# A diffusion layer in fp32 halves: merge's and the output projection's matmuls tied into one order, with some groups of four K tiles out of turn

## The chip, the cores and the metric

The kernel runs on one core of one Trainium2 chip. The metric is the device time of one execution in microseconds (us), as the median of the runs shown. TensorE is PE in what follows (PEld is its weight loads), VectorE is DVE, ScalarE is ACT, GpSimd is POOL, and SyncE's queue of transfers is SP.

## The reference, cut to what matters

One layer over 256 latent tokens and 256 context tokens of width 2048. Its attention branches give `ya` and `yb` (256 x 1024 each); the part that the change touches is the merge and the output projection:

```
g_a, g_b = split(sigmoid(h @ w_gate + b_gate), 2)
mix = (g_a * (ya @ w_proj_gla) + g_b * (yb @ w_proj_diff)) @ w_out
x_new = x + g1 * mix
h2 = modulate(rms_norm(x_new, norm2_w), sh2, sc2)
x_new = x_new + g2 * conv_ffn(h2)          # w_up, conv, silu gate, w_down
```

All of it is fp32. `w_proj_gla` and `w_proj_diff` are 1024 x 2048, `w_out` is 2048 x 2048, `w_up` 2048 x 11264, `w_down` 5632 x 2048.

## The kernel before, in words

Activations lie transposed (128 features by 256 tokens) and are split into a high half, rounded to TensorE's fp32r type, and a low half, the rest. Weights come from HBM in pieces of 128 x 1024 (`fetch`, L225, four buffers `wraw`); `split` (L199) makes of each 128 x 512 the halves `whi` (a copy on ACT, L206) and `wlo` (a subtraction, L213, on DVE or now and then on POOL), four buffers of each. One such 128 x 512 holds four K tiles: a group.

`col_tile` (L238) computes one column tile: 128 output features by 256 tokens, summed over its K tiles. For each K tile there are two matmuls: h (L262), the weight's high half against both halves of the activation (512 columns), and l (L264), the weight's low half against the activation's high half (256 columns). A group of four K tiles has eight matmuls in one of three orders:

```
TURN = "h0 l0 h1 l1 h2 l2 h3 l3".split()
ENDED = "h0 l0 h1 l1 h2 l2 l3 h3".split()
SHIFTED = "h0 h1 l0 h2 l1 h3 l2 l3".split()
```

The instructions are written in program order and a scheduler then sets the order on each engine by its own estimate of times. Where `col_tile` is given orders, its matmuls are tied: each is held behind the one before it in one chain (`chain`, L265 to L268), so that the scheduler can't mix two column tiles. Without orders all groups are TURN but the last, which is ENDED, and the scheduler may move matmuls of the next tile ahead. Before the change only the up and down projections (tiles named `upg`, `upv`, `down`) are tied; out of turn are there the groups of column tiles 8 to 16 of `w_up` and 0 to 2 of `w_down`.

The stages around the change, in order:

- The gates (`gate_tile`), 32 column tiles of `w_gate`, not tied.
- The merge, L1090 to L1107: 16 columns, each with two column tiles of 8 K tiles, `pga` (against `ya`) and `pgb` (against `yb`). ACT copies half of a finished bank to `pt` (L273), DVE adds the other half (L274), the result is multiplied with the gate (L1101, on DVE for `pga`, on POOL for `pgb`), and a column later `merged` adds both (L1086) and splits the sum into the halves of `A[c]` (L231 on ACT, L232 on DVE). The tiles `a0` to `a15` are these `A[c]`.
- The output projection, L1128 to L1152: 16 column tiles `mix` of 16 K tiles. Each needs all of `a0` to `a15`, so its last K tile waits for the last `merged`.
- `up0`, six column tiles of `w_up` side by side (`up`, L1177 to L1179), not tied, while `normed` (L1165 to L1167) makes the new `a0` to `a15`; then `upg` and `upv` column tiles, 41 of each, with the convolution (L1211 to L1214), the gate's silu and product (L1221, L1222) for each pair; then 16 `down` tiles.

Between all this DVE computes modulation vectors: 128 x 1024 pieces of `w_ada` (`araw`, two buffers, transfers issued at L332 on SP) are multiplied with a vector and summed, one dot of L338 each. In the merge there are 12 of them for 16 columns. SP issues all weight transfers in one order.

Of the kernel before, what the change touches and what calls it, by code (L numbers as in the profile page):

```python
# [146 lines left out]
def layer_kernel(tc, I, out):  # L147
# [3 lines left out]
    with es:  # L151
# [82 lines left out]
        TURN = "h0 l0 h1 l1 h2 l2 h3 l3".split()  # L234
        ENDED = "h0 l0 h1 l1 h2 l2 l3 h3".split()
        SHIFTED = "h0 h1 l0 h2 l1 h3 l2 l3".split()

        def col_tile(src, acts, b, orders=None):  # L238

            nk = src.shape[1]
            nq = nk // 4
            tied = orders is not None
            orders = orders or [TURN] * (nq - 1) + [ENDED]
            for k0 in range(0, nk, 8):
                kn = min(8, nk - k0)
                if k0:  # L250
                    flush()
                raw = fetch(src[:, k0:k0 + kn, :].rearrange("p a b -> p (a b)"), kn * P)
                for kk in range(0, kn, 4):
                    whi, wlo = split(raw[:, kk * P:(kk + 4) * P], 4 * P)
                    order = orders[(k0 + kk) // 4]
                    for which in order:
                        j = int(which[1])
                        k = k0 + kk + j
                        sl = slice(j * P, (j + 1) * P)
                        first, last = k == 0 and which == "h0", k >= nk - 4 and which == order[-1]  # L260
                        if which[0] == "h":
                            i = PE.matmul(b.rearrange("p (a b) -> p a b", a=2), whi[:, sl], acts[k], start=first, stop=last)  # L262
                        else:
                            i = PE.matmul(b[:, T:], wlo[:, sl], acts[k][:, 1, :], start=False, stop=last)  # L264
                        if tied:  # L265
                            if chain:
                                after(i, chain[0])
                            chain[:] = [i]  # L268
                    if k0 and not kk:
                        flush(latest)  # L270
# [32 lines left out]
        A, B, C = [], [], []  # L303
# [785 lines left out]

        for c in range(KT):  # L1090
            ba, bb = acc_bank("pga"), acc_bank("pgb")
            col_tile(I["w_proj"][c, :, 0:8, :], yap, ba)
            col_tile(I["w_proj"][c, :, 8:16, :], ybp, bb)
            for j in (c, 16 + c):
                sigs.append(S.activation(gates[j], gates[j], AF.Sigmoid))
                after(sigs[-1], sigm)
                after(sigs[-1], copied[0])
            for b, j in ((ba, c), (bb, 16 + c)):
                t = p3.tile([P, T], F32, tag="pt", bufs=2, name="pt")
                i = added(t, b)  # L1100
                (G if j > c else V).tensor_tensor(gates[j], t, gates[j], op=ALU.mult)  # L1101
                if j == c and c:
                    merged(c - 1, i)
            ada_next(12 / 16)
# [24 lines left out]
        for c in range(KT):  # L1129
            b = acc_bank("mix")  # L1130
            if c < half:
                ada_next(1)
            col_tile(I["w_out"][c], A, b)
            if c == half:
                ada_done(16)
                ada_done(32)
                V.tensor_scalar(a2, adav[:, 32:48], 1.0, None, op0=ALU.add)
                V.tensor_tensor(a2, a2, vcol("norm2", 0, 16), op=ALU.mult)
                V.tensor_scalar(a2, a2, -0.5 / D, None, op0=ALU.mult)
            xr = p3.tile([P, T], F32, tag="xr", bufs=2, name="xr")  # L1140
            nc.scalar.dma_start(xr, I["xl"][:, c, :])
            x1.append(C[c][:, 0, :])
            V.scalar_tensor_tensor(xr, b[:, :T], adav[:, c:c + 1], xr, op0=ALU.mult, op1=ALU.add)
            i = V.scalar_tensor_tensor(x1[c], b[:, T:], adav[:, c:c + 1], xr, op0=ALU.mult, op1=ALU.add)
            if c >= half:
                for k in range(2 * (c - half), 2 * (c - half) + 2):
                    unnormed(k, i, summed)
            sq = p3.tile([P, T], F32, tag="sq2" if c else "sq_sum", bufs=2 if c else 1, name="sq2")
            S.activation(sq, x1[c], AF.Square)
            if c == 0:  # L1150
                sq_sum = sq
            elif c < KT - 1:  # L1152
                summed = G.tensor_tensor(sq_sum, sq_sum, sq, op=ALU.add)
# [43 lines left out]
        with tc.tile_pool(name="ffn", bufs=1) as pf:  # L1197
# [26 lines left out]
                split_act(g[:, 1, :], g[:, 0, :], ug)  # L1224
                gs.append(g)

            def orders(n, nq, first, last):


                shifted = [i for j in range(0, nq * (last - first + 1) - 3, 7) for i in (first * nq + j, first * nq + j + 4)]  # L1230
                q = range(n * nq, (n + 1) * nq)
                return [ENDED if i == (last + 1) * nq - 1 else SHIFTED if i in shifted else TURN for i in q]

            for j in range(UPS // 2):
                gated(j, ups[2 * j], ups[2 * j + 1])
            for j in range(UPS // 2, FT):
# [9 lines left out]
            for c in range(KT):  # L1246
                b = acc_bank("down")
# [21 lines left out]
```

## Time and profile before

| what | value |
|---|---|
| median of 3 runs (lowest, highest) | 1704.58 us (1703.33, 1706.26) |
| the profiled execution: time, span of its profile | 1705.99 us, 1704.2 us |
| PE, PEld, DVE, ACT, POOL busy | 99%, 86%, 73%, 58%, 22% |
| matmuls | 10460 |
| bytes read from HBM | 364.73 MB |

Lines of a timeline give start, duration, engine, source line, operation, output and inputs, and in brackets the idle time before an instruction and what ended it. Successive matmuls overlap: the pace is read from starts, not from durations. DVE and ACT too start an instruction a little before the one ahead has ended. SPq lines are transfers being issued. In a table of windows each row has a stretch of time, its length, and busy time with the number of instructions for each engine, PE first.

### The profile page before, as it was taken

The page shows a single profiled execution, that of the slowest core. Times are in us where ns is not written, and L with a number is a line of the kernel's source. Part 1 is how long each engine was busy: PE and PEld are TensorE (multiplying, and loading weights), DVE is VectorE, ACT ScalarE, POOL GpSimd, SP SyncE. Part 2 cuts the span into 40 slices and gives each one's busy share as a digit, 9 for nine tenths or more (in the row PEclk, how much of TensorE's full clock was granted, in tenths as well). Part 3 has the DMA queues.
Part 4 walks back from the last instruction along what each step waited for, and adds up shares of the span by engine and source line. Part 5 has one row for each costly group of instructions (what it writes and reads, how often), then busy time and mean ns, then how long its engine had stood idle before and what let it go on. Part 6 is the DMA issues. An engine that isn't in the chain of part 4 may idle for free.

```text
span 1704.2 us, 29160 instructions
## 1 busy us (share of the span) xinstructions
PE 1680.4 (99%) x10460; PEld 1461.5 (86%) x10460; DVE 1236.4 (73%) x2314; ACT 983.8 (58%) x1992; POOL 373.4 (22%) x384
## 2 busy tenths in 40 slices
PE   8999999999999999999999999999999999999999
PEld 6779999897887888888888988888888888888887
DVE  5556665867688988788998797777788777644443
ACT  5324554655355777666666676666666666444443
POOL 0002534545110000001213212222222222222222
PEclk9999999999999999999999999999999999999999
DMA  9995532433667554687787666666776666666664
GB/s 384 407 408 182 173 121 90 136 112 124 197 210 234 169 178 161 216 299 271 259 276 259 182 217 220 223 225 226 231 231 225 224 227 225 202 199 195 200 200 135
DMA packets 108451, 368.75 MB, mean 216 GB/s; under 512 B 12176, under 2 KB 17040, under 8 KB 108304
## 3 DMA queue, kind: packets, MB, share of 16 engines
q1 hardware_dynamic: 103264, 362.51, 63.7%
q10 hardware_dynamic: 5040, 4.37, 0.8%
q8 instruction: 82, 1.34, 0.3%
q14 instruction: 65, 0.53, 0.1%
HBM read 364.73 MB, written 2.10 MB: 215 GB/s over the span
## 4 chain that ended last, share of the span: by engine, by line
PE 90%; DVE 5%; DMA 3%; ACT 1%; issue 1%; POOL 0%; DVEq 0%; ACTq 0%
PE down L262 9%; PE upg L262 8%; PE upv L262 8%; PE gate L262 7%; PE sweep L350 5%; PE down L264 5%; PE upg L264 4%; PE upv L264 4%; PE gate L264 4%; PE mix L262 3%; PE ab L350 2%; DMA araw<-in_w_ada 2%; PE mix L264 2%; PE pga L262 2%; PE pgb L262 2%; PE dk L313 1%
## 5 line engine op out<-in xcount | busy, mean ns | idle before, releaser
L206 ACT CAST whi<-wraw 128x512 fp32r<-128x512 f32 (+2 forms) x1004 | 605.6, 608 | 388.5 <-PE down L262 110.5
L213 DVE TENSOR_TENSOR wlo<-wraw,whi 128x512 fp32r<-128x512 f32 (+2 forms) x849 | 588.7, 703 | 236.8 <-ACT whi L206 228.7
L213 POOL TENSOR_TENSOR wlo<-wraw,whi 128x512 fp32r<-128x512 f32 (+1 forms) x155 | 208.2, 1343 | 644.9 <-ACT whi L206 572.2
L262 PE MATMUL down<-g,whi 128*128 128x512 f32 x704 | 243.6, 392 | 0.0
L262 PE MATMUL upg<-a,whi 128*128 128x512 f32 x656 | 229.4, 392 | 0.0
L262 PE MATMUL upv<-a,whi 128*128 128x512 f32 x656 | 229.3, 392 | 0.0
L264 PE MATMUL down<-g,wlo 128*128 128x256 f32 x704 | 195.4, 280 | 0.7 <-DVE wlo L213 0.7
L264 PE MATMUL upg<-a,wlo 128*128 128x256 f32 x656 | 182.8, 280 | 1.0 <-DVE wlo L213 1.0
L264 PE MATMUL upv<-a,wlo 128*128 128x256 f32 x656 | 182.8, 280 | 0.0
L262 PE MATMUL gate<-a,whi 128*128 128x512 f32 x512 | 179.4, 396 | 0.0
L338 DVE CUSTOM_DVE_ANT_0 araw<-araw,cb 128x1024 f32<-128x1024 f32 x128 | 163.7, 1282 | 15.2 <-DMA araw<-in_w_ada 15.2
L262 PEld LDWEIGHTS down<-g,whi 128*128 128x128 f32 x704 | 131.0, 187 | 28.3
L262 PEld LDWEIGHTS upv<-a,whi 128*128 128x128 f32 x656 | 122.4, 187 | 26.8
L262 PEld LDWEIGHTS upg<-a,whi 128*128 128x128 f32 x656 | 122.4, 187 | 26.7
L264 PE MATMUL gate<-a,wlo 128*128 128x256 f32 x512 | 140.9, 285 | 0.5 <-DVE wlo L213 0.5
L264 PEld LDWEIGHTS down<-g,wlo 128*128 128x128 f32 x704 | 132.9, 189 | 1.9 <-DVE wlo L213 1.0
L264 PEld LDWEIGHTS upg<-a,wlo 128*128 128x128 f32 x656 | 123.9, 189 | 2.2 <-DVE wlo L213 1.6
L264 PEld LDWEIGHTS upv<-a,wlo 128*128 128x128 f32 x656 | 123.9, 189 | 0.5
L262 PEld LDWEIGHTS gate<-a,whi 128*128 128x128 f32 x512 | 94.3, 188 | 19.3 <-issue 0.4
L264 PEld LDWEIGHTS gate<-a,wlo 128*128 128x128 f32 x512 | 96.5, 188 | 6.9 <-issue 1.5
L262 PE MATMUL mix<-a,whi 128*128 128x512 f32 x256 | 88.8, 397 | 0.0
L264 PE MATMUL mix<-a,wlo 128*128 128x256 f32 x256 | 69.3, 281 | 1.0 <-DVE wlo L213 1.0
(332 smaller groups left out, 3346.0 us busy)
## 6 DMA issues: line engine op xcount, KB each, us to landing
wraw<-in_w_up SPq DMA_DIRECT2D x164, 512.0 KB, 4.4
araw<-in_w_ada SPq DMA_DIRECT2D x128, 512.0 KB, 5.0
wraw<-in_w_down SPq DMA_DIRECT2D x80, 512.0 KB, 3.9
ada<-in_w_ad SPq DMA_DIRECT2D x64, 512.0 KB, 9.8
wraw<-in_w_gate SPq DMA_DIRECT2D x64, 512.0 KB, 4.2
wraw<-in_w_in SPq DMA_DIRECT2D x58, 512.0 KB, 3.9
wraw<-in_w_proj SPq DMA_DIRECT2D x32, 512.0 KB, 4.5
wraw<-in_w_out SPq DMA_DIRECT2D x32, 512.0 KB, 4.8
```

Of the source, the lines that this page charges most:

```text
L206: copied[0] = S.copy(hi[:, :n], raw)
L213: i = e.tensor_tensor(lo[:, :n], raw, hi[:, :n].bitcast(F32), op=ALU.subtract)
L262: i = PE.matmul(b.rearrange("p (a b) -> p a b", a=2), whi[:, sl], acts[k], start=first, stop=last)
L264: i = PE.matmul(b[:, T:], wlo[:, sl], acts[k][:, 1, :], start=False, stop=last)
L313: PE.matmul(o, whi[:, sl], hi[k], start=first and j == 0, stop=False)
L338: i = V.tensor_tensor_reduce(raw, raw, cb[:, q * 1024:(q + 1) * 1024], 1.0, 0.0, op0=ALU.mult, op1=ALU.add, accum_out=ada2[:, j, q:q + 1])
L350: return kept(PE.matmul(*args, **kw))
```

## The change

The function `orders`, which so far stood in the part of the up and down projections, moves ahead of `col_tile`, and the merge's and the output projection's column tiles are given orders by it. `orders(n, nq, first, last)` returns the orders of column tile n with nq groups: between the tiles first and last the groups at distances 0, 4, 7, 11, 14 and so on from the first are SHIFTED, the very last group of tile last is ENDED, all others are TURN.

```
-            col_tile(I["w_proj"][c, :, 0:8, :], yap, ba)
-            col_tile(I["w_proj"][c, :, 8:16, :], ybp, bb)
+            col_tile(I["w_proj"][c, :, 0:8, :], yap, ba, orders(2 * c, 2, 2, 18))
+            col_tile(I["w_proj"][c, :, 8:16, :], ybp, bb, orders(2 * c + 1, 2, 2, 18))
...
-            col_tile(I["w_out"][c], A, b)
+            col_tile(I["w_out"][c], A, b, orders(c, 4, 2, 7))
...
+        def orders(n, nq, first, last):
+            shifted = [i for j in range(0, nq * (last - first + 1) - 3, 7) for i in (first * nq + j, first * nq + j + 4)]
+            q = range(n * nq, (n + 1) * nq)
+            return [ENDED if i == (last + 1) * nq - 1 else SHIFTED if i in shifted else TURN for i in q]
```

In the merge this makes groups 4, 8, 11, 15, 18, 22, 25, 29, 32 and 36 of 64 SHIFTED and 37 ENDED; in the output projection groups 8, 12, 15, 19, 22 and 26 of 64 SHIFTED and 31 ENDED. Every column tile so far ended in an ENDED group. No instruction is added or removed; SP's and POOL's orders stay as they were, while those of PE, DVE and ACT change from the first `pga` tile to the first `upg` tiles. In the changed kernel the lines between `col_tile` and the old place of `orders` have numbers higher by 7.

PE at the end of the first output tile. `mix_9955` is column tile 0, `mix_10017` column tile 1; `wlo_10000` and `whi_9999` are tile 0's last group, `a15_1450` its last K tile's activation. Before:

```order
L264 MATMUL mix_9955<-a14_1380,wlo_10000 128x256
L264 MATMUL mix_10017<-a0_219,wlo_10024 128x256
L262 MATMUL mix_10017<-a1_330,whi_10023 128x512
L264 MATMUL mix_10017<-a1_330,wlo_10024 128x256
L262 MATMUL mix_10017<-a2_402,whi_10023 128x512
L264 MATMUL mix_10017<-a2_402,wlo_10024 128x256
L262 MATMUL mix_10017<-a3_481,whi_10023 128x512
L264 MATMUL mix_10017<-a3_481,wlo_10024 128x256
L262 MATMUL mix_10017<-a4_560,whi_10035 128x512
L264 MATMUL mix_9955<-a15_1450,wlo_10000 128x256
L264 MATMUL mix_10017<-a4_560,wlo_10036 128x256
```

The same place in the changed kernel:

```order
L271 MATMUL mix_9955<-a14_1380,wlo_10000 128x256
L269 MATMUL mix_9955<-a15_1450,whi_9999 128x512
L271 MATMUL mix_9955<-a15_1450,wlo_10000 128x256
L269 MATMUL mix_10017<-a0_219,whi_10023 128x512
L271 MATMUL mix_10017<-a0_219,wlo_10024 128x256
L269 MATMUL mix_10017<-a1_330,whi_10023 128x512
```

Before, three groups of tile 1 stand ahead of tile 0's last high product with `a15`, which follows only after the l of tile 1's K tile 11; now both products with `a15` stand ahead of all of tile 1.

DVE at the same place. `pt_9942` belongs to the last `pgb`, the C15 rows to the last column's gates (the second of them is the last `merged`), `araw_9947` is a dot of the modulation vectors, `wlo_10024`, `wlo_10036` and `wlo_10050` are the first three groups of output tile 1. Before:

```order
L1101 TENSOR_TENSOR C15_8738<-pt_9935,C15_8738 128x256
L274 TENSOR_TENSOR pt_9942<-pgb_9880,pt_9942 128x256
L232 TENSOR_TENSOR a14_1380<-C14_8618,a14_1380 128x256
L213 TENSOR_TENSOR wlo_10000<-wraw_9985,whi_9999 128x512
L338 ISA araw_9947,ada2_77<-araw_9947,cb_76 128x1024
L338 ISA ada2_77 128x1
L213 TENSOR_TENSOR wlo_10024<-wraw_10021,whi_10023 128x512
L1086 TENSOR_TENSOR C15_8738<-C15_8738 128x256
L213 TENSOR_TENSOR wlo_10036<-wraw_10021,whi_10035 128x512
L213 TENSOR_TENSOR wlo_10050<-wraw_10047,whi_10049 128x512
L232 TENSOR_TENSOR a15_1450<-C15_8738,a15_1450 128x256
```

The same place in the changed kernel:

```order
L1108 TENSOR_TENSOR C15_8738<-pt_9935,C15_8738 128x256
L213 TENSOR_TENSOR wlo_10000<-wraw_9985,whi_9999 128x512
L345 ISA araw_9947,ada2_77<-araw_9947,cb_76 128x1024
L345 ISA ada2_77 128x1
L281 TENSOR_TENSOR pt_9942<-pgb_9880,pt_9942 128x256
L213 TENSOR_TENSOR wlo_10024<-wraw_10021,whi_10023 128x512
L232 TENSOR_TENSOR a14_1380<-C14_8618,a14_1380 128x256
L213 TENSOR_TENSOR wlo_10036<-wraw_10021,whi_10035 128x512
L1093 TENSOR_TENSOR C15_8738<-C15_8738 128x256
L213 TENSOR_TENSOR wlo_10050<-wraw_10047,whi_10049 128x512
L232 TENSOR_TENSOR a15_1450<-C15_8738,a15_1450 128x256
```

The add that belongs to the last `pgb` and the low half of `a14` have moved behind the dot; the last `merged` stands one `wlo` later.

DVE where `up0` ends and the `upg` tiles begin. `h2t_11551` and `a15_1450` are the two steps of the last `normed`; the L1190 rows empty the six banks of `up0`; `wlo_11671` and `wlo_11683` are the first two groups of the first `upv` tile. Before:

```order
L1165 SCALAR_TENSOR_TENSOR h2t_11551<-C15_8738,a2_9954,n2y_11063 128x256
L213 TENSOR_TENSOR wlo_11645<-wraw_11642,whi_11644 128x512
L1190 TENSOR_TENSOR C15_8738<-up0_11026,n2y_11063 128x256
L1190 TENSOR_TENSOR C14_8618<-up1_11027,n2y_11063 128x256
L1190 TENSOR_TENSOR C13_8501<-up2_11028,n2y_11063 128x256
L1167 SCALAR_TENSOR_TENSOR a14_1380<-h2t_11547,adav_78,a14_1380 128x256
L1190 TENSOR_TENSOR C12_8381<-up3_11029,n2y_11063 128x256
L1190 TENSOR_TENSOR C11_8264<-up4_11030,n2y_11063 128x256
L1190 TENSOR_TENSOR C10_8081<-up5_11031,n2y_11063 128x256
L1167 SCALAR_TENSOR_TENSOR a15_1450<-h2t_11551,adav_78,a15_1450 128x256
```

The same place in the changed kernel, from the fifth of the rows that empty `up0`:

```order
L1197 TENSOR_TENSOR C11_8264<-up4_11030,n2y_11063 128x256
L1172 SCALAR_TENSOR_TENSOR h2t_11551<-C15_8738,a2_9954,n2y_11063 128x256
L1197 TENSOR_TENSOR C10_8081<-up5_11031,n2y_11063 128x256
L1174 SCALAR_TENSOR_TENSOR a14_1380<-h2t_11547,adav_78,a14_1380 128x256
L213 TENSOR_TENSOR wlo_11671<-wraw_11668,whi_11670 128x512
L1219 SCALAR_TENSOR_TENSOR C1_6299<-C15_8738,vec_71,C1_6299 128x255
L213 TENSOR_TENSOR wlo_11683<-wraw_11668,whi_11682 128x512
L1219 SCALAR_TENSOR_TENSOR C2_6577<-C14_8618,vec_71,C2_6577 128x255
L1221 SCALAR_TENSOR_TENSOR C1_6299<-C15_8738,vec_71,C1_6299 128x255
L1174 SCALAR_TENSOR_TENSOR a15_1450<-h2t_11551,adav_78,a15_1450 128x256
```

The last `normed` has moved back behind the emptying of `up0`, two `wlo` groups and three steps of the convolution. Further on, the row of the second `upg` tile's first low half (`wlo_11742`) and that of its third (`wlo_11768`) stand four rows later than before.

More of the change, by code (lines that the diff above doesn't have):

```diff
@@ L236, in layer_kernel, with col_tile @@
         SHIFTED = "h0 h1 l0 h2 l1 h3 l2 l3".split()
-        def col_tile(src, acts, b, orders=None):
+        def orders(n, nq, first, last):
+            shifted = [i for j in range(0, nq * (last - first + 1) - 3, 7) for i in (first * nq + j, first * nq + j + 4)]
+            q = range(n * nq, (n + 1) * nq)
+            return [ENDED if i == (last + 1) * nq - 1 else SHIFTED if i in shifted else TURN for i in q]
+        def col_tile(src, acts, b, turns=None):
             nk = src.shape[1]
             nq = nk // 4
-            tied = orders is not None
-            orders = orders or [TURN] * (nq - 1) + [ENDED]
+            tied = turns is not None
+            turns = turns or [TURN] * (nq - 1) + [ENDED]
             for k0 in range(0, nk, 8):
@@ L254, in col_tile @@
                     whi, wlo = split(raw[:, kk * P:(kk + 4) * P], 4 * P)
-                    order = orders[(k0 + kk) // 4]
+                    order = turns[(k0 + kk) // 4]
                     for which in order:
@@ L1225, in gated @@
                 gs.append(g)
[L1227 to L1232, printed above, removed]
             for j in range(UPS // 2):
```

## The prediction

> **What bounds the kernel now.** I began with the page: span, busy times, the chain that ended last and the groups with their idle time.
>
> ```profile
> span 1704.2 us, 29160 instructions
> PE 1680.4 (99%) x10460; PEld 1461.5 (86%) x10460; DVE 1236.4 (73%) x2314; ACT 983.8 (58%) x1992; POOL 373.4 (22%) x384
> PE 90%; DVE 5%; DMA 3%; ACT 1%; issue 1%; POOL 0%; DVEq 0%; ACTq 0%
> L264 PE MATMUL upg<-a,wlo 128*128 128x256 f32 x656 | 182.8, 280 | 1.0 <-DVE wlo L213 1.0
> L264 PE MATMUL mix<-a,wlo 128*128 128x256 f32 x256 | 69.3, 281 | 1.0 <-DVE wlo L213 1.0
> ```
>
> PE is the bound, and it hardly waits: around the change there is 1.0 us of idle time in the output projection and 1.0 us in the first up tiles. The number of matmuls doesn't change, so there are two things to ask: at what pace do they follow each other in each order, and where does PE wait that did not wait before. For the pace I took four windows of 45 us each: merge, output projection, up tiles 8 to 16 (tied, with SHIFTED groups), and later up tiles (tied, all TURN).
>
> ```profile
> 800.00:845.00 45.00, 45.00 (x260) 39.33 (x259) 44.66 (x85) 31.65 (x74) 10.60 (x9) 1.00 0.80 258
> 885.00:930.00 45.00, 45.00 (x256) 39.01 (x255) 39.60 (x70) 25.07 (x47) 15.79 (x16) 1.00 0.84 289
> 1050.00:1095.00 45.00, 45.00 (x260) 39.29 (x259) 35.87 (x63) 28.74 (x57) 11.18 (x8) 1.00 0.67 225
> 1100.00:1145.00 45.00, 45.00 (x261) 39.70 (x260) 35.79 (x63) 29.18 (x58) 11.08 (x8) 1.00 0.68 227
> ```
>
> PE's first number is full in all four and the granted clock is 1.00, yet the counts differ: 256 matmuls in the output projection, 260 in merge and with SHIFTED groups, 261 in the tied tiles after them. The order of high and low products thus has a price without any wait. Two timelines of PE, the starts of low products in strict turn, before (up tiles) and after the region with SHIFTED groups, show it:
>
> ```profile
> 1030.08 0.28 PE L264 MATMUL upv<-a,wlo 128*128 128x256 f32 x1
> 1030.43 0.28 PE L264 MATMUL upv<-a,wlo 128*128 128x256 f32 x1
> 1030.79 0.28 PE L264 MATMUL upv<-a,wlo 128*128 128x256 f32 x1
> 1031.13 0.28 PE L264 MATMUL upv<-a,wlo 128*128 128x256 f32 x1
> ```
> ```profile
> 1200.15 0.28 PE L264 MATMUL upg<-a,wlo 128*128 128x256 f32 x1
> 1200.50 0.28 PE L264 MATMUL upg<-a,wlo 128*128 128x256 f32 x1
> ```
>
> The same TURN order runs either in a cycle of three pairs (steps 0.35, 0.36, 0.34 us) or evenly at 0.35 or a little less; which one depends on what came before. SHIFTED groups lead out of the cycle, and after the ENDED group at tile 16 the even pace holds without SHIFTED groups.
>
> **The change part by part.** First the pace, which is all that the change means to move.
>
> *Merge*, 16 columns in 90 us: from the pace of 260 to between 260 and 261 in 45 us, so at most 90 x 1/261 = 0.35 us, less a little for column 0, which is TURN throughout and may run in the cycle. *Output projection*: a tile of 32 matmuls takes 32 x 45/256 = 5.63 us in the cycle, 5.54 at 260 and 5.52 at 261. Tiles 2 to 7 get SHIFTED groups (6 x 0.09 = 0.54), tiles 8 and 9 the even pace (2 x 0.11 = 0.22); the last six hardly gain, since 117 matmuls in 20 us (row below) is no slower than 261 in 45. A wait of 0.2 us that PE has at 931 us may throw tiles 11 to 15 back into the cycle, which would cost 0.1 us each. I take 0.6 us (0.2 to 0.9).
>
> ```profile
> 940.00:960.00 20.00, 20.00 (x117) 17.48 (x116) 17.27 (x31) 11.85 (x23) 8.19 (x16) 1.00 0.60 190
> ```
>
> *The tie at the start of the output projection.* This is where I looked longest: the first tile needs `a15`, the last thing that merge makes. PE, DVE, POOL, SP and the chain of waits there:
>
> ```profile
> 876.29 0.28 PE L264 MATMUL mix<-a,wlo 128*128 128x256 f32 x1
> 877.59 0.38 PE L264 MATMUL mix<-a,wlo 128*128 128x256 f32 x1 [1.02 <-DVE wlo L213]
> ```
> ```profile
> 866.55 1.27 DVE L213 TENSOR_TENSOR wlo<-wraw,whi 128x512 fp32r<-128x512 f32 x1
> 867.74 1.21 DVE L338 CUSTOM_DVE_ANT_0 araw<-araw,cb 128x1024 f32<-128x1024 f32 x1
> ```
> ```profile
> 872.84 0.41 DVE L274 TENSOR_TENSOR pt<-pgb,pt 128x256 f32<-128x256 f32 x1
> 873.18 0.41 DVE L232 TENSOR_TENSOR a<-C,a 128x256 fp32r<-128x256 f32 x1
> 873.33 0.85 POOL L1101 TENSOR_TENSOR C<-pt,C 128x256 f32<-128x256 f32 x1 [6.06 <-DVE pt L274]
> 873.51 1.23 DVE L213 TENSOR_TENSOR wlo<-wraw,whi 128x512 fp32r<-128x512 f32 x1
> 875.70 1.22 DVE L338 CUSTOM_DVE_ANT_0 araw<-araw,cb 128x1024 f32<-128x1024 f32 x1 [0.96 <-DMA araw<-in_w_ada]
> 876.85 0.69 DVE L213 TENSOR_TENSOR wlo<-wraw,whi 128x512 fp32r<-128x512 f32 x1
> 877.46 0.42 DVE L1086 TENSOR_TENSOR C<-C 128x256 f32<-128x256 f32 x1
> 877.79 1.28 DVE L213 TENSOR_TENSOR wlo<-wraw,whi 128x512 fp32r<-128x512 f32 x2
> 879.00 0.42 DVE L232 TENSOR_TENSOR a<-C,a 128x256 fp32r<-128x256 f32 x1
> ```
> ```profile
> 860.00 8.17 SPq L227 DMA_DIRECT2D wraw<-in_w_out  x4
> 868.99 1.47 SPq L332 DMA_DIRECT2D araw<-in_w_ada  x2
> ```
> ```profile
> 868.99 6.69 DMA araw<-in_w_ada
> ```
>
> Now, PE comes to tile 0's K tile 14 at 876.29, goes on with tile 1, waits 1.02 us for its first low half, and works on while `a15` is finished at 879.42. Tied, it must wait for `a15` itself. And DVE reaches `a15` by another road: the dot, which waited 0.96 us for its transfer, now stands ahead of the last `pt` add, and behind that add come a POOL product, the last `merged` and `a15`. From the dot's start T I step by the starts above: dot 1.15 (875.70 to 876.85), `pt` 0.34, `wlo` 1.2 (beside POOL's product it took 1.23 instead of 0.69), low half of `a14` 0.33, `wlo` 0.6, `merged` 0.33, `wlo` 0.6, `a15` 0.42: T + 5.0. T is the landing of the transfer. It was 875.70, 6.69 us after its issue at 868.99, when the dot of 867.74 had freed its buffer. The changed order takes the `pt` add from ahead of that dot, and the `wlo` there, which took 1.27, runs with no POOL product beside it (the add that starts it comes later): the dot starts when ACT's copy allows, by my estimate 1.5 us earlier, 866.2. So T is between 874.2 and 875.70, and I take 874.5, since SP's issues all move with that dot. PE then goes on at 879.5 (879.2 to 880.7, or less by up to 0.6 if POOL's product falls beside no `wlo`), against 877.59: 1.9 us later, and with one matmul more to do (481 left before, 482 now), 0.1. What merge gained is lost in this wait, which begins earlier and ends at T + 5.0 whatever PE does. Term: +2.0 us (+1.0 to +3.2).
>
> [...]
>
> *The first up tiles.* The scheduler's order of DVE changes down to here.
>
> ```profile
> 998.31 1.08 DVE L1190 TENSOR_TENSOR C<-up,n2y 128x256 f32<-128x256 f32 x3
> 999.30 0.61 DVE L1167 SCALAR_TENSOR_TENSOR a<-h2t,adav,a 128x256 fp32r<-128x256 f32 x1
> 1000.84 0.47 DVE L1167 SCALAR_TENSOR_TENSOR a<-h2t,adav,a 128x256 fp32r<-128x256 f32 x1
> 1001.23 0.68 DVE L213 TENSOR_TENSOR wlo<-wraw,whi 128x512 fp32r<-128x512 f32 x1
> ```
> ```profile
> 1003.01 0.39 PE L262 MATMUL upg<-a,whi 128*128 128x512 f32 x1
> 1008.92 0.39 PE L262 MATMUL upg<-a,whi 128*128 128x512 f32 x1
> 1009.66 0.39 PE L264 MATMUL upg<-a,wlo 128*128 128x256 f32 x1 [0.36 <-DVE wlo L213]
> ```
>
> Times here are those of before; all of it shifts with what went ahead. `a15` was finished at 1001.31, and PE used it at 1003.01 (the K tile 15 of the first `upg`): 1.7 us of slack. Now `h2t` of `a15` no longer stands ahead of the emptying (0.4 less), and ahead of `a15` come two `wlo` (0.6 each) and three steps of the convolution (0.4 each, the step from 1000.84 to 1001.23 for the same operation), with `h2t` again: 0.4 less and 2 x 0.6 + 3 x 0.4 + 0.4 = 2.8 more, 1003.7, and some tenths for ACT's half of `normed`, which moves back as well. So PE waits about 1 us for `a15`. Part of it was to come anyway: it waited at 1008.92 for the low half that ended at 1009.61, and that row now stands four rows later among much the same work. Four rows of 0.33 to 0.4 are 1.5 us, less the three steps of `normed` and emptying that had stood ahead: I take 0.9 us as what is late in the end (0 to 1.5).
>
> Sum: -0.6 + 2.0 + 0.9 = +2.3 us on a span of 1704.2 us. The profiled execution took 1705.99 us, 1.4 above the median of the three; I put the difference on the median: 1704.58 + 2.3 = 1706.9 us. About 0.2%, 3.4 us, is what a measurement of this kernel can tell from no change; the three runs lie 2.9 us apart. So this is "no change", on the slow side.
>
> **The rivals.** *The waits don't grow* (0.18). The transfer lands by 872.5, when DVE is ready for the dot, and ACT and DVE keep `a15` of the up tiles in time. Then PE waits at the start of the output projection for T + 5.0 = 877.5, as before, and only the gains stay: 0.6 and up to 0.4 of merge, 1703.6 us. For it: SP issues earlier. Against it: 6.69 us of landing time, and four weight transfers just ahead.
>
> *The order of halves is free* (0.10). The pace is set by the columns alone, or the groups placed here miss the point at which the cycle breaks: the ENDED group of the merge stands directly behind a SHIFTED one, that of the projection five groups behind, in the up tiles three. The gain is then 0, and the sum 2.9: 1707.5 us. [...]
>
> *Slower: the late landing* (0.15). T stays at 875.70 or comes later because the transfers before it share the same queues; this decides from T = 875.5 on. PE goes on at 880.7, 3.1 us late, and the first up tiles cost their 1.5: 3.1 + 0.1 + 1.5 - 0.6 = +4.1, 1708.7 us.
>
> *Slower: the even pace is lost behind the up tiles* (0.05). If the new history leaves tile 17 and all after it in the cycle, the 65 up tiles that follow pay 0.11 us each, 7 us: 1711.6 us. Against it: SHIFTED groups lead out of the cycle from wherever it began.
>
> **How the numbers follow.** The forecast has 0.52, with 1705.0 to 1708.6 of its own from its bounds. With the rivals the range is 1703.4 to 1709.2; outside lie the last rival and the far ends of two others. Slower by over 3.4 us (above 1708.0): the last two rivals, less some of the landing's, and a tail of the forecast, 0.23. Faster by over 3.4 us would need more than all of PE's waits there: 0.03. The rest, 0.74, is no change.
>
> **What would show it.** In the profile after: counts of 260 or 261 in windows of the projection's tiles 2 to 9 (gain right); PE waiting 3 us or more ahead of tile 0's K tile 15, with DVE idle ahead of the dot (second term); a PE wait for `a15` in the first `upg` tile (third). The prediction is wrong if PE's wait at the start of the projection is still about 1 us, or if the tiles behind tile 8 still show 256 in 45 us.

## The result, and the profile after

| | before | after |
|---|---|---|
| median (lowest, highest) of 10 runs each | 1704.94 us (1703.33, 1706.54) | 1709.45 us (1707.40, 1712.10) |
| the profiled execution: time, span | 1705.99, 1704.2 us | 1708.13, 1706.3 us |

The changed kernel is slower by 0.3%: the ratio is 1.0029, with a 95% interval of 1.002 to 1.0037. The forecast of 1706.9 us was too low, and its range (to 1709.2) ends just below the median. The two profiled executions are only 2.1 us apart, close to the forecast's 2.3; the medians are 4.5 apart. So these two traces don't hold the whole of it, and the experiments have more traces of both kernels. An execution that took 1830.30 us at a lower granted clock (0.851), one of ten with the projection tied alone, is left out of that kernel's median and ratio.

The page's first lines after, and the windows that the prediction had shown of before (merge, projection, its later tiles, and the two stretches of up tiles):

```profile
span 1706.3 us, 29219 instructions
PE 1680.0 (98%) x10460; PEld 1461.1 (86%) x10460; DVE 1234.4 (72%) x2314; ACT 985.1 (58%) x1992; POOL 369.0 (22%) x384
```
```profile
800.00:845.00 45.00, 45.00 (x259) 39.33 (x258) 43.76 (x85) 31.32 (x73) 8.18 (x8) 1.00 0.77 259
885.00:930.00 45.00, 45.00 (x261) 39.39 (x260) 39.72 (x69) 23.74 (x44) 13.38 (x16) 1.00 0.82 276
940.00:960.00 20.00, 20.00 (x117) 17.66 (x116) 17.05 (x30) 11.38 (x21) 9.37 (x20) 1.00 0.63 204
1050.00:1095.00 45.00, 45.00 (x261) 39.26 (x260) 35.88 (x64) 28.81 (x57) 10.93 (x8) 1.00 0.68 224
1100.00:1145.00 45.00, 45.00 (x261) 39.67 (x261) 36.06 (x65) 28.82 (x57) 11.07 (x8) 1.00 0.69 225
```

Compare the first numbers in brackets, PE's matmuls. The projection went from 256 to 261 matmuls in 45 us, as the prediction says; the merge, where it saw up to one more, has one less (259 against 260).

The start of the output projection, PE and then DVE:

```profile
876.65 0.28 PE L271 MATMUL mix<-a,wlo 128*128 128x256 f32 x1
877.71 0.50 PE L269 MATMUL mix<-a,whi 128*128 128x512 f32 x1 [0.78 <-DVE a L232]
878.05 0.28 PE L271 MATMUL mix<-a,wlo 128*128 128x256 f32 x1
879.59 0.50 PE L269 MATMUL mix<-a,whi 128*128 128x512 f32 x1 [1.26 <-DVE a L232]
```
```profile
874.62 1.23 DVE L345 CUSTOM_DVE_ANT_0 araw<-araw,cb 128x1024 f32<-128x1024 f32 x1 [0.34 <-DMA araw<-in_w_ada]
...
875.77 0.42 DVE L281 TENSOR_TENSOR pt<-pgb,pt 128x256 f32<-128x256 f32 x1
876.11 0.68 DVE L213 TENSOR_TENSOR wlo<-wraw,whi 128x512 fp32r<-128x512 f32 x1
876.71 0.95 DVE L232 TENSOR_TENSOR a<-C,a 128x256 fp32r<-128x256 f32 x1
877.58 0.68 DVE L213 TENSOR_TENSOR wlo<-wraw,whi 128x512 fp32r<-128x512 f32 x1
878.18 0.41 DVE L1093 TENSOR_TENSOR C<-C 128x256 f32<-128x256 f32 x1
878.52 0.68 DVE L213 TENSOR_TENSOR wlo<-wraw,whi 128x512 fp32r<-128x512 f32 x1
879.12 0.41 DVE L232 TENSOR_TENSOR a<-C,a 128x256 fp32r<-128x256 f32 x1
```

This is the chain that the prediction stepped through: the dot starts when its row lands (T = 874.62), then `pt`, `wlo`, the low half of `a14`, `wlo`, `merged`, `wlo`, the low half of `a15`. PE, tied, waits twice in it, for `a14` and for `a15`, and goes on at 879.59 = T + 4.97. Before, PE waited once there, 1.02 us for a `wlo`. All of PE's waits for one line in the projection and the up tiles:

```profile
PE mix L269 <- DVE a L232: 2.0, 2, 1.3
PE upg L269 <- DVE a L1174: 1.2, 1, 1.2
PE upg L271 <- DVE wlo L213: 0.9, 1, 0.9
PE mix L271 <- DVE wlo L213: 0.2, 1, 0.2
```

The columns are us in total, times, longest. The wait for `a` at L1174 is the `a15` of the first up tile, the prediction's third step.

### The profile page after: what moved, and what is told of

Its sections match the earlier page's. It is cut to its first block, busy times and chain, and to the rows that moved or that the text cites. A ratio compares the mean times of both kernels' runs of the same rounds, so it can differ in the third digit from the quotient of the medians.

```text
span 1706.3 us, 29219 instructions
## 1 busy us (share of the span) xinstructions
PE 1680.0 (98%) x10460; PEld 1461.1 (86%) x10460; DVE 1234.4 (72%) x2314; ACT 985.1 (58%) x1992; POOL 369.0 (22%) x384
## 4 chain that ended last, share of the span: by engine, by line
PE 90%; DVE 5%; DMA 2%; ACT 2%; issue 1%; POOL 0%; ACTq 0%; DVEq 0%
PE down L269 9%; PE upg L269 9%; PE upv L269 9%; PE gate L269 7%; PE sweep L357 5%; PE down L271 5%; PE upg L271 4%; PE upv L271 4%; PE gate L271 4%; PE mix L269 3%; PE ab L357 2%; PE pgb L269 2%; PE pga L269 2%; PE mix L271 1%; DMA araw<-in_w_ada 1%; PE dk L320 1%
```

## The experiments

Each kernel was compared with the kernel before on the same chip. Ratios are to it, with 95% intervals.

### Which part of the change costs the time

Three kernels, each with one edit against the changed kernel. The merge tied alone (the projection is free again):

```
-            col_tile(I["w_out"][c], A, b, orders(c, 4, 2, 7))
+            col_tile(I["w_out"][c], A, b)
```

> Only the merge's products are tied; the output projection's are left free as in the kernel before. Theory A (the loss stands at the start of the projection, where tied products wait in turn for a14 and a15): the products of the second tile cover these waits again, PE's idle time at the first projection tile falls from 2.6 us to 1.3 us or less, and the time is within 1.2 us of the kernel before's 1704.9. Rival B (the loss comes from the merge's pace: its tied columns go at 5606 ns for 32 matmuls where the kernel before had 5593, or from what it does to DVE's order): most of the 4.5 us stays, 1708 to 1710.

Measured: 1704.72 us, ratio 0.9999 (0.999 to 1.0008). No loss that the times show, so rival B falls. (In the one trace the merge took 91.48 us, 0.8 more than before.)

The projection tied alone:

```
-            col_tile(I["w_proj"][c, :, 0:8, :], yap, ba, orders(2 * c, 2, 2, 18))
-            col_tile(I["w_proj"][c, :, 8:16, :], ybp, bb, orders(2 * c + 1, 2, 2, 18))
+            col_tile(I["w_proj"][c, :, 0:8, :], yap, ba)
+            col_tile(I["w_proj"][c, :, 8:16, :], ybp, bb)
```

> Only the output projection's products are tied; the merge is that of the kernel before. DVE's row then has the last addition pt ahead of the waiting dot (as before), and a14 too, but the merge of the last column and a15 behind it. Theory A: PE is held once, for a15, 1 to 2 us, and again at the first up tiles; 1706.5 to 1709.5, most of the 4.5 us. Rival B (the merge): within 0.7 us of 1704.9.

Measured: 1709.63 us, the median of nine executions, ratio 1.0027 (1.0017 to 1.0036); a little above the expected 1709.5. Tying the projection alone brings the whole loss.

Only the projection's first tile free:

```
-            col_tile(I["w_out"][c], A, b, orders(c, 4, 2, 7))
+            col_tile(I["w_out"][c], A, b, orders(c, 4, 2, 7) if c else None)
```

> As the changed kernel, but the first tile of the projection is left free, so that the scheduler puts the second tile's products between those that wait for a14 and a15; the other fifteen tiles stay tied. Theory A: the waits of the start are covered and the pace of the projection (0.6 us) stays; the first up tiles still cost their 0.9 us: 1704.5 to 1706.5. Rival B: 1708 to 1710. Rival C (the loss comes from the first up tiles alone, whose slack the tied projection has taken): 1707 to 1709, with PE's waits for DVE's a there as long as in the changed kernel.

Measured: 1704.71 us, ratio 0.9999 (0.999 to 1.0008). Freeing one tile of sixteen takes the loss away. PE's waits in its trace:

```profile
PE upg L269 <- DVE a L1174: 1.2, 1, 1.2
PE mix L271 <- DVE wlo L213: 0.2, 1, 0.2
```

The wait for `a15` of the merge is gone; that for the up tiles' `a15` is as long as in the changed kernel, and yet the loss is gone, so rival C falls too. The edit did more than free a tile, though: the wait for `wlo` at the second `upg` tile, 0.9 us, is gone as well, since the scheduler wrote DVE's rows in another order there, and that `wlo` stands three rows earlier. In this trace the projection's first 64 products took 11.43 us, 3.1 less than the mean of four traces of the changed kernel (the table below), and the first 96 products of the up tiles 18.89 us, 0.8 less.

### The dot ahead of a15, and its landing

The merge asks for its 12 rows of `w_ada` one a column, in columns 0 to 11:

```
-            ada_next(12 / 16)
+            ada_next(1 if c < 12 else 0)
```

> As the changed kernel, but the merge asks for its 12 adaptive rows one a column in columns 0 to 11 instead of 0.75 a column, so that the row of the dot that stands ahead of the last pt and a15 on DVE has landed some 20 us before. DVE's order there stays as it is. Theory A with a varying landing: the dot starts when DVE reaches it, about 870 us on the changed kernel's scale, a15 comes 5.0 us later, PE's 2.6 us of waits at the first projection tile go, and the median falls by 2 to 4 us, to 1705.5 to 1707.5, with a smaller spread. Theory A without it (the waits are of DVE's order alone): PE is still held there by over 1.5 us, and the time stays at 1708.5 to 1710. Rival B: 1708.5 to 1710 with PE not held at the start.

Measured: 1707.33 us, ratio 1.0014 (1.0005 to 1.0023), 1706.05 to 1709.63. In its trace the dot waits for no transfer. PE's waits for `a` don't go, as expected, but shrink: it still waits 0.96 us for `a15`, and an additional wait of 1.0 us for `wlo` stands in the merge. The same without touching the merge, the projection's rows asked for a tile later:

```
-            if c < half:
+            if 0 < c <= half:
                 ada_next(1)
```

> As the changed kernel, but the projection's calls for adaptive rows stand before tiles 1 to 8 instead of 0 to 7. The dot that stands on DVE ahead of the last pt is then one whose row was asked for a column earlier, in the merge; DVE's order around it stays. Theory A with a varying landing: no wait for a transfer on DVE there, PE is held for a15 by some 1 us as with the early row, and since the merge isn't touched the median is 1705.5 to 1707, at or below that run's 1707.3. Theory A without it (DVE's order alone): 1708.5 to 1710.

Measured: 1707.52 us, ratio 1.0015 (1.0006 to 1.0024). The expectation's upper bound of 1707 was too low; the mechanism shows in DVE's rows, the dot's and those of `pt` and `a15`:

```profile
873.01 1.21 DVE L345 CUSTOM_DVE_ANT_0 araw<-araw,cb 128x1024 f32<-128x1024 f32 x1
...
874.15 0.42 DVE L281 TENSOR_TENSOR pt<-pgb,pt 128x256 f32<-128x256 f32 x1
...
877.51 0.41 DVE L232 TENSOR_TENSOR a<-C,a 128x256 fp32r<-128x256 f32 x1
```

No wait in brackets: the dot starts when DVE comes to it, 1.46 us after the projection's first product (871.55) and not 2.79; `a15` begins 4.5 us after the dot, as in the changed kernel (874.62 to 879.12), and PE waits once (0.96 us) instead of twice. About half of the loss goes with the landing. The projection's first 64 products took 12.42 us in this trace, within what the kernel before shows (11.41 to 12.43); what is left of the loss stands at the up tiles, as the next experiment shows.

Last, the dot itself put behind `a15` on DVE, by a dependency of that one dot on the low half of `a15` (`last_a`); all products stay tied:

```
-        def ada_next(n):
+        def ada_next(n, behind=None):
...
-                    ada_dot()
+                    i = ada_dot()
+                    if behind is not None:
+                        after(i, behind)
...
-                ada_next(1)
+                ada_next(1, last_a if c == 1 else None)
```

> As the changed kernel with all its products tied; only the dot of the late row is put behind a15 on DVE (a dependency on a15's low half). Theory A: a15 comes some 3.3 us after the merge's last product, before the tied products ask for it; PE isn't held at the first projection tile, and the time is that of the run with the first tile free, 1704 to 1705.5: the tie costs nothing there without the dot. Rival (DVE's order of pt, a14, merged, a15 holds PE even without the dot): still held by over 0.7 us, 1706 to 1708.

Measured: 1707.73 us, ratio 1.0012 (1.0003 to 1.0021); the rival's time, not mine. Its trace:

```profile
871.93 0.41 DVE L281 TENSOR_TENSOR pt<-pgb,pt 128x256 f32<-128x256 f32 x1
...
875.28 0.41 DVE L232 TENSOR_TENSOR a<-C,a 128x256 fp32r<-128x256 f32 x1
875.62 1.21 DVE L345 CUSTOM_DVE_ANT_0 araw<-araw,cb 128x1024 f32<-128x1024 f32 x1
```
```profile
875.75 0.51 PE L269 MATMUL mix<-a,whi 128*128 128x512 f32 x1 [0.73 <-DVE a L232]
```

The dot does stand behind, and `a15` comes 3.4 us after `pt` begins. PE still waits 0.73 us. At the start of the projection most of the loss is gone (12.30 us for its first 64 products, against means of 14.50 in the changed kernel and 11.99 before, from the table below), but the first 96 products of the up tiles took 20.61 us, against 19.72 in the first trace of the changed kernel: DVE's rows stand in another order there, and PE's one long wait for `wlo`, 1.0 us instead of 0.9, comes 16 products later; that this makes the 0.9 us is not shown. (Both kernels with the earlier row show 20.61 us there too, and the kernel before 18.60.) So taking the dot away cures most of the start, and part of that is given back at the up tiles. The profiled execution is the shortest of its eleven, 1705.41 us.

### Where the rest of the 4.5 us is: more traces

Three more traces of the changed kernel and three of the kernel before, nothing edited.

> The changed kernel once more, for its trace. Its times spread over 4.7 us (1707.4 to 1712.1) where the kernel before's spread over 3.2, and the trace at hand is of one of its shorter executions. Theory A with a varying landing: the dot that waits for its adaptive row starts at another moment T after the projection's first product than the 2.8 us of the trace at hand, PE goes on 5.0 us after T, and the projection's length follows T. Rival: T stays within 0.3 us of 2.8 us after the first product, and a difference in time stands in another stage.

> As the run before: the changed kernel, for its trace. Theory A with a varying landing: T moves and the projection's length with it. Rival: T stays, and what differs in time differs in another stage.

> The changed kernel for a fourth trace. From the merge's start to the last instruction the three traces so far have 925.4, 925.4 and 928.2 us. Theory D with a varying landing: 925 to 926.5 where the row lands 2.8 to 3.5 us after the projection's first product and the clock stays at 1.00, 927.5 to 929 with PE's clock near half after the waits; nothing in between. Rival E: lengths in between, with the clock at 1.00.

Measured: 1708.77, 1712.02 and 1709.99 us. The dot started 3.20, 3.53 and 2.74 us after the projection's first product (2.79 in the first trace), and PE went on at T + 4.97, 4.96 and 4.96. The landing moves, and PE with it. From the merge's start to the end the three took 925.36, 928.19 and 926.63 us. The last is 0.1 us above what theory D gives for a full clock; it holds 0.5 us in the projection's last tiles that D doesn't have (the table below). The second is longer by more than its landing:

```profile
879.49 0.50 PE L269 MATMUL mix<-a,whi 128*128 128x512 f32 x1 [1.52 <-DVE a L232]
879.82 0.28 PE L271 MATMUL mix<-a,wlo 128*128 128x256 f32 x1
881.36 0.50 PE L269 MATMUL mix<-a,whi 128*128 128x512 f32 x1 [1.26 <-DVE a L232]
...
882.96 0.63 PE L269 MATMUL mix<-a,whi 128*128 128x512 f32 x1
883.38 0.41 PE L271 MATMUL mix<-a,wlo 128*128 128x256 f32 x1
883.60 0.63 PE L269 MATMUL mix<-a,whi 128*128 128x512 f32 x1
```
```profile
877.00:879.00 2.00, 0.97 (x6) 0.60 (x4) 2.00 (x5) 0.62 (x1) 0.95 (x1) 1.00 0.95 340
...
881.50:883.50 2.00, 2.00 (x8) 1.66 (x9) 1.45 (x3) 1.04 (x2) 0.00 (x0) 0.61 0.60 213
883.50:885.50 2.00, 2.00 (x9) 1.71 (x8) 1.80 (x4) 0.62 (x1) 0.00 (x0) 0.53 0.61 201
885.50:888.00 2.50, 2.50 (x17) 2.19 (x16) 0.84 (x2) 0.95 (x2) 0.00 (x0) 1.00 0.76 224
```

The third column from the right is the granted clock: after the two waits it falls to half, for 3.4 us (0.61 and 0.53 are means of windows that hold some full clock; the trace's own record of the clock has 0.50 from 881.95 to 885.37), and a high product takes 0.63 us instead of 0.40. The first 64 products took 16.06 us, against 13.81 to 14.26 in the other three traces: 2.1 us for the fall of the clock and the later row together, 0.4 to 0.8 of them the row's.

The changed kernel's 13 times fall into two groups: nine from 1707.40 to 1709.99, four from 1711.42 to 1712.10, of which one is this trace. Each execution's mean granted clock is on record too. A fall of 3.4 us to half brings it to 0.999 by my sum (1.7 of 1710 us), and 0.999 is what that trace's execution has. Three executions of the kernel before have 0.999 too (1703.62, 1705.83 and 1705.86 us); theirs may come from the program's end, where in the first trace of that kernel the clock is at half from 1704.26, 4.1 us after PE's last product began. 1.000 leaves no room for a fall of 3.4 us. All four of the upper group have 0.999, and of the lower nine only one. To test the clock, spare products were put on PE in the waits of the first tile, 3 ahead of those of `a14` and 5 ahead of those of `a15`, into a bank that nothing reads:

```
+                        for _ in range(fill.get(k, 0) if which[0] == "h" else 0):
+                            i = PE.matmul(spare.rearrange("p (a b) -> p a b", a=2), whi[:, sl], acts[0], start=True, stop=True)
+                            after(i, chain[0])
+                            chain[:] = [i]
```

> As the changed kernel, with 8 more products of a weight tile at hand and a0 on PE in the first projection tile, 3 ahead of a14's and 5 ahead of a15's, into a spare bank that nothing reads; some 0.23 us each, so shorter in sum than the waits that they stand in. Theory D (in some executions PE's two waits together are so long that the granted clock falls to about half for over 3 us after them, at a cost of some 1.9 us): no execution falls into the upper group that the changed kernel shows (1711.4 to 1712.1 in 4 of 12 executions, the other 8 from 1707.4 to 1709.5), and the median is 1708 to 1709.5. Rival E (no such fall, or a rare one that means nothing; the long executions are those whose row landed latest): the times stay spread as they were, a quarter or more of them over 1711.

Measured: 1708.55 us, ratio 1.0015 (1.0006 to 1.0023), 1707.32 to 1710.65. None of 11 executions is in the upper group, and all 11 have a mean clock of 1.000. With more work on PE the kernel was, if anything, faster, though `a15` comes no earlier; the two intervals overlap a little.

The contrary, a longer wait (four multiplications by 1.0 on DVE in the last `merged`), and that wait with 13 spare products in it:

```
+            for _ in range(4 if c == KT - 1 else 0):
+                V.tensor_scalar(gates[c], gates[c], 1.0, None, op0=ALU.mult)
```

> As the changed kernel, with four multiplications by 1.0 of the last merged tile in place on DVE ahead of a15, so that a15 comes some 1.3 us later. Theory D: the longer wait brings the half clock in most executions: 1709.45 + 1.3 + (1.9 in the two thirds that didn't have it) = 1712 to 1713, and the trace shows a granted clock near 0.55 after the wait. Rival E: only the 1.3 us are added, 1710.5 to 1711.2, with the clock at 1.00.

> As the run with the four multiplications, with 13 spare products on PE in the waits (3 ahead of a14's, 10 ahead of a15's, some 3 us in all). Theory D: a15 comes as late, but PE is busy meanwhile, the clock stays at 1.00, and the time is 1709 to 1711, 2 us or more below the run without them. Rival E: within 0.7 us of the run without them, or slower where the spare products themselves hold PE up.

Measured: 1711.18 us, ratio 1.003 (1.002 to 1.004), and 1709.68 us, ratio 1.0021 (1.0012 to 1.003). PE without the spare products, two of its rows and a window behind them:

```profile
878.70 0.50 PE L269 MATMUL mix<-a,whi 128*128 128x512 f32 x1 [0.97 <-DVE a L232]
...
882.33 0.64 PE L269 MATMUL mix<-a,whi 128*128 128x512 f32 x1 [3.01 <-DVE a L232]
```
```profile
883.50:885.50 2.00, 2.00 (x8) 1.71 (x7) 1.97 (x4) 0.53 (x2) 0.00 (x0) 0.50 0.09 27
```

And with them:

```profile
878.23 2.47 PE L269 MATMUL spare<-a,whi 128*128 128x512 f32 x10
881.40 0.50 PE L273 MATMUL mix<-a,whi 128*128 128x512 f32 x1 [0.69 <-DVE a L232]
```
```profile
883.50:885.50 2.00, 2.00 (x13) 1.76 (x12) 1.95 (x5) 1.25 (x3) 0.00 (x0) 1.00 0.57 168
```

In the traces theory D holds: 0.50 of the clock where PE stood, 1.00 where it worked through the same wait, eight matmuls in two us against thirteen. It holds in all executions: the mean clock is 0.998 or 0.999 in all nine with the longer wait and 1.000 in all 11 with the spare products. In the times it holds by sign and not by size: the difference is 1.5 us where over 2 were expected, the two intervals overlap, and the longer wait alone came out at 1711.18, the upper end of what rival E gave.

The kernel before:

> The kernel before once more, for its trace. Theory F (the trace of the kernel before at hand is of an execution with long waits, and that of the changed kernel of one with short waits, so that their difference of 2.1 us is too small): between the merge's start and the last instruction it takes 922.5 to 923.5 us where the trace at hand has 923.9, with a wait for wlo at the first projection tiles below 1.3 us. Rival: 923.7 to 924.2, the waits as in the trace at hand, and the other 2.4 us of the changed kernel come from executions of its own that no trace shows yet.

> As the run before: the kernel before, for its trace. Theory F: 922.5 to 923.5 us from the merge's start to the last instruction. Rival: 923.7 to 924.2.

> As the two runs before: the kernel before, for its trace. Theory F: 922.5 to 923.5 us from the merge's start to the last instruction. Rival: 923.7 to 924.2.

Measured: from the merge's start to the end 922.85, 923.54 and 922.31 us (923.92 in the first trace). The first lies in theory F's 922.5 to 923.5, the others 0.04 above and 0.2 below it. F holds for its part: the trace on which the prediction rests is the longest of four. Its wait of 1.02 us for `wlo` at the start of the projection is 0.46 and 0.78 in two others and absent in the third. The row is also late before, but there PE has the second tile's products to do:

```profile
876.84 0.39 PE L264 MATMUL mix<-a,wlo 128*128 128x256 f32 x1 [0.46 <-DVE wlo L213]
```

With four traces of each kernel, the mean length of each stage (lowest to highest in brackets), counted between starts of PE's products. Each stretch ends where both kernels have done the same products. The last product of the projection is no such place: in the changed order the two products of `ss`, the sums for the second normalization, stand ahead of it (it starts at 965.03), where before they followed it (962.78). After, then before:

```profile
962.83 0.59 PE L1163 MATMUL ss<-sq,ones 128*128 128x256 f32 x2
965.03 0.28 PE L271 MATMUL mix<-a,wlo 128*128 128x256 f32 x1
```
```profile
962.78 0.40 PE L262 MATMUL mix<-a,whi 128*128 128x512 f32 x1
964.08 0.60 PE L1156 MATMUL ss<-sq,ones 128*128 128x256 f32 x2
```

| stretch | before | after | difference |
|---|---|---|---|
| start to the merge's first product | 780.30 (780.01 to 780.83) | 781.54 (780.93 to 782.04) | +1.24 |
| merge | 90.68 | 90.87 (90.82 to 90.92) | +0.19 |
| projection, first 64 products | 11.99 (11.41 to 12.43) | 14.50 (13.81 to 16.06) | +2.51 |
| products 64 to 352 | 51.04 | 50.55 | -0.49 |
| product 352 to the first of the up tiles | 63.00 | 63.19 (62.94 to 63.45) | +0.19 |
| first 96 products of the up tiles | 18.60 (18.58 to 18.62) | 19.72 (19.69 to 19.76) | +1.12 |
| to the end | 687.83 | 687.57 | -0.26 |
| span | 1703.45 | 1707.95 | +4.49 |

The sum is as large as the difference of the medians, 4.5 us, but the two are not made alike. One of the four traces after has the fall of the clock; the median after lies between two executions whose clock was 1.000 (1709.40 and 1709.50), and the six executions of the ten with 1.000 have a median of 1709.3. So the fall, some 0.5 us in the table's mean, is hardly in the median. Without that trace the span's difference is 3.7 us, 1.1 of them ahead of the merge.

### A version from the parts

The merge free, the projection tied from its second tile, and the first pair of up tiles free:

```
-            col_tile(I["w_out"][c], A, b, orders(c, 4, 2, 7))
+            col_tile(I["w_out"][c], A, b, orders(c, 4, 2, 7) if c else None)
...
-                col_tile(I["w_up"][2 * j - UPS], A, bg, orders(2 * j - UPS, KT // 4, 8, 16))
+                col_tile(I["w_up"][2 * j - UPS], A, bg, orders(2 * j - UPS, KT // 4, 8, 16) if j > UPS // 2 else None)
```

> A version built from the parts: the merge free as in the kernel before, the projection tied from its second tile on, and the up tiles tied from their second pair on (the first pair free). Theory A: the projection's pace gives 0.6 us, the first pair's wait for a15 (1.2 us) is covered by products of the pair's second tile, the merge's slower pace (0.2 us) goes: 1702.8 to 1704.2 against 1705.1. Rival: the wait for wlo at the second up tile takes the place of that for a15, and the time is that of the run with the first tile free, 1704.7.

Measured: 1704.59 us, ratio 0.9995 (0.9985 to 1.0004). The wait for the up tiles' `a15` is gone from its trace, and the first 96 products of the up tiles took 18.35 us. But the median is above the expected 1704.2 and close to the rival's 1704.7; the gain is within what the measurement can tell from nothing. And with the projection's last five tiles free too:

```
-            col_tile(I["w_out"][c], A, b, orders(c, 4, 2, 7) if c else None)
+            col_tile(I["w_out"][c], A, b, orders(c, 4, 2, 7) if 0 < c < 11 else None)
```

> The version built from the parts (merge free, first up pair free, projection tied from its second tile), with the projection's last five tiles left free too, so that only tiles 2 to 11 are tied. If the last five tiles' loss in the changed kernel (28.8 to 29.3 us from product 352 to the last, against 28.3 in the kernel before) comes from their tie: that stretch is back at 28.3 us, tiles 3 to 11 keep 50.6, and the median falls by 0.4 us below that of the version built from the parts, to some 1.3 us under the kernel before: 1703.5 to 1704.4. If it comes from DVE's order (the additions and the wait for wlo there) and not from the tie: 28.8 us, and no gain.

Measured: 1705.16 us, ratio 1.0000 (0.9991 to 1.0009). The expected 1703.5 to 1704.4 is missed. The stretch from product 352 to the projection's last is back at 28.29 us, as expected, but that isn't the tie's doing: in this order the two products of `ss` follow the last product again. Counted to the first product of the up tiles, where both have done the same, it is 62.96 us, against 62.94 in the version before it and 63.00 in the kernel before. The premise, that the tie of the last five tiles loses 0.4 us in every trace, rested on a count of unlike things; the 0.45 us of two traces of the changed kernel (63.45) this one trace can't settle. No version here is faster than the kernel before by more than the measurement's uncertainty.

## Why the prediction was wrong

The sign, the place and the mechanism were right; the sum was too small, by 2.2 us against the traces' difference of 4.5. Three steps fell short: the projection's pace brought half of what it was counted for, the wait at the start was priced by its length alone, without the clock that it can cost, and the part ahead of the merge was put at nothing, where 1.24 us stand whose cause stays open. Another 0.4 us is the forecast's base: three executions with a median of 1704.58 us, where ten gave 1704.94. Step by step:

- *Merge* ("at most 0.35 us", lost in the wait): it gained nothing. Its tied columns settle at 5606 ns for 32 products, where the free ones of before took 5593. +0.19 us. The step failed in carrying the up tiles' pace over to other orders of the same rule.
- *Projection's pace* (-0.6 us, "the last six hardly gain"): -0.49 us up to product 352, as forecast. From there to the up tiles it is -0.06 us in two traces and +0.45 in the other two, where after a wait of 0.2 us for `wlo` at tile 10, which all four have, PE was back in the cycle of three pairs (5649 to 5661 ns for 32 products instead of 5547). The prediction named this fall and priced it at 0.1 us a tile, which is what it measured, but took off only 0.16 us for it (0.76 to 0.6); the mean of this step is -0.3, not -0.6.
- *The tie at the start* (+2.0 us): T + 5.0 was right to 0.04 us in all four traces. The estimate that the dot ahead would start 1.5 us earlier was too large: counted from the projection's first product it started 1.0 us earlier (4.21 us ahead of it instead of 3.22), and its `wlo` did wait for ACT's copy, 0.17 us. T, forecast 3.5 us after that product (874.5 against 870.96), came at 2.74 to 3.53. In the three traces with the full clock the first 64 products took 13.98 us, 2.0 more than before's mean. The sign named for this step, a wait of 3 us or more ahead of K tile 15, did not come as such: the waits were 0.7 to 1.5 us ahead of `a14`'s and 1.26 us ahead of `a15`'s product. That the net is just the forecast's 2.0 is in part luck: PE went on 7.7 to 8.5 us after the first product, where the forecast's 879.5 means 8.5, and before's own wait, from which the step counted, was the longest of four. What the step lacked is the clock: in the trace of 1712.02 us the two waits, 1.52 and 1.26, cost another 1.3 to 1.7 us after they had ended. With it the term is +2.5 in the mean of the traces.
- *First up tiles* (+0.9 us): PE waits 1.2 us for `a15` there, as forecast; the net is +1.12, a little more.
- *The sum.* From the merge on, the four terms give 0.2 - 0.3 + 2.5 + 1.1 = 3.5, less 0.3 of spread in the later stages: +3.2 us, against a forecast of +2.3. The other +1.24 us stands ahead of the merge, where each engine has the same instructions in the same order in both kernels. Some 0.7 us of it arises in an early stage (tiles `dvb`, around 515 to 540 us), where PE's waits for `whi` and `wlo` sum to 0.6 to 1.1 us in the traces before and to 0.9 to 1.8 after, and 0.25 in the gates. In the 11 traces of other kernels here that share these instructions, most of them with the tied projection, the merge starts between 778.73 and 781.38, at 780.05 in the mean, close to the 780.30 of the kernel before. That speaks for chance, and so does the free first tile, which removes all of the median's 4.5 us without touching that part. But if it was chance in four traces, then the medians hold a like amount that no stage here explains. It stays open.
- *The reference.* The prediction set a sum made against one execution onto the median. That execution was the longest of four in just the stage at issue.

Of the rivals, the late landing came nearest in its number (1708.7 us), but its condition didn't come: T = 875.5 is 4.5 us after the projection's first product in the trace before, and no trace after has more than 3.53. It counts 1.2 us for a landing that late, and nothing ahead of the merge, where 1.24 us came: that its number is near is luck. "The order of halves is free" fell (256 to 261 in 45 us).

## What to carry to other kernels

A scheduler's freedom to run the next tile's products was worth most here at the first tile behind a stage's last result; if tiles are to be tied, tie those behind it, not that one. Before tying PE to a chain on another engine, look what stands ahead of the chain's last steps there: here an unrelated dot waited 0.3 to 1.1 us for its transfer, and PE went on 4.96 or 4.97 us after the landing in all four traces, early or late. Price a wait of PE's not by its length alone: in one trace two of them close together, 1.52 and 1.26 us, were followed by 3.4 us at a clock of 0.50; spare products in the longer wait kept it at 1.00 (by the times 1.5 us cheaper than standing, with intervals that overlap). And when stages of two kernels are compared, let them end where both have done the same work: a change of order can move instructions across a stage's last one.

## What the runs showed of the hardware

- The granted clock fell to half after 1.52 and 1.26 us of idle PE with one pair of products between them (2.78 us in sum; the changed kernel's trace of 1712.02 us), and after 0.97 and 3.01 (the longer wait without spare products). It stayed at 1.00 after 0.78 and 1.26 (2.04 us; the first trace), and with the spare products in the longer wait, where 0.20 and 0.69 us of idleness were left. After 1.19 and 1.26 (2.45 us; the trace of 1708.77 us) high products went on at 0.40 us, and the mean clock was 1.000. It was at half for 3.42 us in the one case; in the other the windows (0.76 and 0.50 over 2 us each, 0.91 over the next 2.5) make 3.4. What decides between 2.45 and 2.78 us of idleness, and whether the sum is what counts, is not shown.
- In the four traces of the changed kernel these two waits sum to 2.0 to 2.8 us, and the clock fell in the one with the most. That fits that only some of its executions pay: four of 13 are in the upper group.
- The strict turn of high and low products ran at three paces with the granted clock at 1.00: 5547 ns for 32 products in the later up tiles and the `down` tiles of both kernels, 5649 to 5661 in the projection, 5606 in the changed kernel's merge. Which one held differed with what came before: behind the wait of 0.2 us at the projection's tile 10 it was 5547 in two traces of the changed kernel and 5649 to 5661 in the other two.
